# Gated linear attention by 128-token blocks, with the chunks' decays in the queries and their factors made for two heads at once

## The chip, the cores and the metric

The kernel runs on one core of a Trainium2 chip. The time is that of one execution on the device, in microseconds (us); lower is better. All data are float32; products with the large weights are made as three products of float32 parts that were split in two ("h" and "l" tiles).

## The reference

Two layers of an encoder on 272 tokens (16 meta tokens and 256 others), width 1024. In each layer four token mixers run in parallel on one input projection: A (differential attention), B (gated linear attention), C (latent attention), D (windowed attention). Their outputs are gated and merged, and a gated MLP follows. The change lies in mixer B, four heads with 64 key and 128 value channels, run forward and backward over chunks of 64 tokens:

```python
def _gla_direction(q, k, v, log_a):          # v: 128 channels, q and k: 64
    q, k, log_a, v = [by chunks of B_CHUNK = 64]
    b = jnp.cumsum(log_a, axis=2)            # within a chunk
    b_end = b[:, :, -1]
    q_dec = q * jnp.exp(b)
    k_in = k * jnp.exp(-b)
    k_out = k * jnp.exp(b_end[:, :, None] - b)
    att = jnp.einsum('bnthd,bnshd->bnhts', q_dec, k_in) * causal
    o = jnp.einsum('bnhts,bnshe->bnthe', att, v)
    d_state = jnp.einsum('bnshd,bnshe->bnhde', k_out, v)
    def step(S, inp):
        dS, dec = inp
        return dec[..., None] * S + dS, S
    _, S_start = lax.scan(step, S0, (d_state, jnp.exp(b_end)))
    o = o + jnp.einsum('bnthd,nbhde->bnthe', q_dec, S_start)
```

The sum of both directions is normalised over each head's 128 channels and multiplied by a gate. The 272 tokens fall into five chunks: the 16 meta tokens (with padding), and four of 64.

## The kernel before

Activations stand transposed, channels on the 128 partitions and the 272 tokens along the free dimension. A head of mixer B has its 64 forward channels on partitions 0 to 63 and its 64 backward channels on 64 to 127, so that one instruction works on both directions.

The work is written as generators. `interleave(main, n_main, n_fill, fill)` runs `main` step by step and puts `n_fill/n_main` steps of `fill` behind each. In the first stage of a layer `main` is `comp_b1` (decays, with the pair `N_B1`) and then `comp_b2` (the attention itself, `N_B2`), and `fill` is `proj_b_vr` and `proj_a`: projections of the input (tile `pj`), 24 products of 272 columns (258 for some in layer 1) for each block of 128 output channels. Every projection needs its weights split by ScalarE (`wh`, line 221) and by VectorE (`wl`, line 221) from a chunk that arrives by DMA (`raw`); three `raw` and five `wh`/`wl` buffers rotate, the split runs two chunks ahead, and three PSUM banks rotate for `pj`. The framework's scheduler then lays out one fixed order of instructions for each engine; each engine works through its own order and waits by semaphores where an input isn't there.

Mixer B by step, per head h:

- `comp_b1`, first loop: `gpre` (gate logits), Abs, Exp and Ln on ScalarE. Second loop: two scans on VectorE (`x1`), their exponentials on ScalarE (`x3`, `x2`), four small copies of chunk-end decays into `dec` (lines 749 to 752), `ks` and `qs` multiplied with the exponentials, and `ko` (in the tile `x1`): the keys times their chunk's decay (lines 755, 756).
- `keys(h)`: three transposes of `ko` (tile `tk`), copied by ScalarE into `kt` (lines 771, 772).
- `states(h)`: five products `d` (`kt` by values `bvt`), one per chunk, 16 or 64 rows high; two copies and six recursions (line 793) give the state at the start of each chunk, `sst`.
- `scores(h)`: per direction two products of 128 columns and one of 16 (tile `at`, 64 rows high), masks (lines 809, 810) and sums (811, 812) on VectorE, giving `am`.
- `outputs(h)`: `poB`, three products `bvt` by `am` and five `sst` by `qs`, one for each chunk; then squares and `norm(h)` (`ps_B`).

`keys(0)` is the first step of `comp_b2`, `states(0)` the second. The queries of mixer A (`aq`, four blocks) are projected at that time; VectorE reads each block's `pj` (line 544), and ScalarE and VectorE split it (`qmAh`, `qh`, lines 313 and 314).

## Time and profile before

| | |
|---|---|
| median of 3 runs | 1157.58 us (1155.28 to 1157.81) |
| profiled execution, its own time | 1157.4 us |
| its span, first to last instruction | 1155.5 us |
| TensorE matmul busy / weight load busy | 98% / 94% of the span |
| VectorE / ScalarE / GpSimd busy | 82% / 64% / 1% |
| mean granted TensorE clock | 0.997 |

Durations below are of the profiled execution. Matmul rows give start and duration; products follow each other more closely than their durations, so what one costs TensorE is the distance from its start to that of the next. A float32 product that isn't split is recorded as two instructions ("x10" are five products), a split one as one, a transpose as one.

### The profile page before, as it was taken

To read this page: it belongs to the slowest core of one execution; us is meant where nothing else is said; L and a number is where in the kernel's file an instruction comes from. 1 tells how busy PE (TensorE), PEld (TensorE's weight loads), DVE (VectorE), ACT (ScalarE), POOL (GpSimd) and SP (SyncE) were. 2 spreads that over 40 slices of the span, in tenths; PEclk is the share of its full clock that TensorE was granted. 3 is DMA by queue.
4 is the path that set the end of the run, shared out by engine and by line. 5 is a ranking of instruction groups with operands and counts; after the bars stand their busy time and mean duration, and the time that the engine had idled before them with its cause. 6 is when DMAs were issued, how large, how long until landed. Compare 5 with 4: busy or idle time off the path is not lost.

```text
span 1155.5 us, 22869 instructions
## 1 busy us (share of the span) xinstructions
PE 1126.9 (98%) x8686; PEld 1082.9 (94%) x8686; DVE 953.0 (82%) x2153; ACT 743.0 (64%) x1579; POOL 10.5 (1%) x40
## 2 busy tenths in 40 slices
PE   8999999999999999999999999999999999999997
PEld 8989899999999999999999898999999999999986
DVE  7986997898977799995479869978999778999843
ACT  7545886577765767664457447865777657776632
POOL 1000000000000000000000000000000000000000
PEclk9999999999999999999999999999999999999999
DMA  7632454435656356555546424544356463655552
GB/s 261 217 125 92 127 153 144 141 120 142 153 151 201 122 171 201 182 173 168 175 145 220 146 77 125 152 158 152 115 148 169 161 231 102 205 197 191 188 186 74
DMA packets 60914, 183.71 MB, mean 159 GB/s; under 512 B 10443, under 2 KB 17739, under 8 KB 60420
## 3 DMA queue, kind: packets, MB, share of 16 engines
q1 hardware_dynamic: 60148, 181.34, 51.0%
q8 instruction: 68, 1.11, 0.4%
q10 hardware_dynamic: 656, 0.91, 0.2%
q14 instruction: 42, 0.34, 0.1%
HBM read 180.01 MB, written 2.21 MB: 158 GB/s over the span
## 4 chain that ended last, share of the span: by engine, by line
PE 75%; DVE 14%; ACT 5%; issue 3%; DMA 2%; SPq 0%; DVEq 0%; ACTq 0%
PE pj L183 47%; PE dn L183 6%; PE dt L183 5%; PE br L183 5%; DVE wl L221 4%; DMA raw<-wst 2%; ACT wh L221 1%; PE poB L183 1%; PE sc L183 1%; PE at L183 1%; PE poD L183 1%; PE tpp L186 1%; PE d L183 1%; DVE sw L956 1%; PE qu L183 1%
## 5 line engine op out<-in xcount | busy, mean ns | idle before, releaser
L183 PE MATMUL pj<-xh,wh 128*128 128x272 f32 (+1 forms) x1888 | 546.1, 291 | 4.8 <-ACT xh L352 3.9
L183 PE MATMUL pj<-xl,wh 128*128 128x272 f32 (+1 forms) x1888 | 540.4, 287 | 0.0
L183 PE MATMUL pj<-xh,wl 128*128 128x272 f32 (+1 forms) x1888 | 539.8, 287 | 0.0
L221 ACT CAST wh<-raw 128x1024 fp32r<-128x1024 f32 (+2 forms) x322 | 332.7, 1035 | 220.7 <-PE pj L183 94.6
L221 DVE TENSOR_TENSOR wl<-raw,wh 128x1024 fp32r<-128x1024 f32 (+2 forms) x322 | 387.1, 1205 | 96.9 <-ACT wh L221 93.9
L183 PEld LDWEIGHTS pj<-xh,wh 128*128 128x128 f32 x1888 | 354.1, 188 | 10.6 <-ACT xh L352 5.0
L183 PEld LDWEIGHTS pj<-xl,wh 128*128 128x128 f32 x1888 | 356.1, 189 | 1.5 <-issue 0.5
L183 PEld LDWEIGHTS pj<-xh,wl 128*128 128x128 f32 x1888 | 355.7, 188 | 0.4
L1320 ACT ACTIVATE cv<-u,pc 128x272 f32<-128x272 f32 (+1 forms) x88 | 52.8, 605 | 11.3 <-DVE u L1318 11.0
L183 PE MATMUL dn<-ah,wh 128*128 128x272 f32 x176 | 51.0, 290 | 0.0
L183 PE MATMUL dn<-al,wh 128*128 128x272 f32 x176 | 50.7, 288 | 0.0
L183 PE MATMUL dn<-ah,wl 128*128 128x272 f32 x176 | 50.5, 287 | 0.0
L609 ACT ACTIVATE p<-p,st 128x272 f32<-128x272 f32 x68 | 35.1, 517 | 14.8 <-DVE st L607 14.6
L1324 DVE SCALAR_TENSOR_TENSOR cv<-u,pc,cv 128x271 f32<-128x271 f32 (+1 forms) x88 | 43.1, 490 | 1.8
L1322 DVE SCALAR_TENSOR_TENSOR cv<-u,pc,cv 128x271 f32<-128x271 f32 (+1 forms) x88 | 43.0, 488 | 1.2 <-ACT cv L1320 0.9
L1171 DVE TENSOR_TENSOR gt<-pj,rs_x 128x272 f32<-128x272 f32 (+1 forms) x64 | 27.5, 429 | 18.6 <-PE pj L183 18.3
L1318 DVE TENSOR_TENSOR u<-pj,rs_x 128x272 f32<-128x272 f32 (+1 forms) x88 | 37.0, 427 | 0.0
L183 PE MATMUL dt<-wh,al 128*128 128x512 f32 x88 | 34.8, 395 | 0.0
L183 PE MATMUL dt<-wh,ah 128*128 128x512 f32 x88 | 34.7, 395 | 0.0
L183 PE MATMUL dt<-wl,ah 128*128 128x512 f32 x88 | 34.5, 392 | 0.0
L183 PEld LDWEIGHTS dn<-ah,wh 128*128 128x128 f32 x176 | 33.1, 188 | 0.0
L183 PEld LDWEIGHTS dn<-al,wh 128*128 128x128 f32 x176 | 33.1, 188 | 0.0
(385 smaller groups left out, 1922.7 us busy)
## 6 DMA issues: line engine op xcount, KB each, us to landing
raw<-wst SPq DMA_DIRECT2D x306, 512.0 KB, 3.7
raw<-wst SPq DMA_DIRECT2D x12, 384.0 KB, 3.2
bD<-bvec SPq DMA_DIRECT2D x16, 256.0 KB, 5.1
bA<-bvec SPq DMA_DIRECT2D x8, 400.0 KB, 5.4
hT<-hT SPq DMA_DIRECT2D x1, 1088.0 KB, 6.6
h_dram<-hT SPq DMA_DIRECT2D x1, 1088.0 KB
hT<-h_dram SPq DMA_DIRECT2D x1, 1088.0 KB, 6.1
raw<-wst SPq DMA_DIRECT2D x4, 256.0 KB, 4.7
```

Of the source, the lines that this page charges most:

```text
L183: self.note(nc.tensor.matmul(*args, **kw))
L186: self.note(nc.tensor.transpose(*args, **kw))
L221: pair = S.copy(wh[:, c], raw[:, c]), V.tensor_sub(wl[:, c], raw[:, c], wh[:, c].bitcast(F32))
L609: S.activation(p, p, AF.Exp, scale=-1.0, bias=st[:, 0:1], accum_out=st[:, 1:2])
L956: V.tensor_mul(sw[a:a + 32, c0:], src[z:z + 32, c0:], C("sin", z, z + 32)[:, c0:])
L1171: V.tensor_mul(f[:, ct:T], (yield from pj(ct))[:, ct:T], RS[:, ct:T])
L1318: V.tensor_mul(u_[:, ct:T], ps[:, ct:T], RS[:, ct:T])
L1320: S.activation(t[:, cd:T], u_[:, cd:T], AF.Identity, scale=PCc("cw1", c), bias=PCc("cb", c))
L1322: V.scalar_tensor_tensor(t[:, lo:T], u_[:, lo - 1:T - 1], PCc("cw0", c), t[:, lo:T], ALU.mult, ALU.add)
L1324: V.scalar_tensor_tensor(t[:, cd:T - 1], u_[:, cd + 1:T], PCc("cw2", c), t[:, cd:T - 1], ALU.mult, ALU.add)
```

## The change

Mixer B no longer makes a state for each chunk of 64 tokens, but only for each block of 128 (and the meta tokens' block): three blocks instead of five chunks. What lies between the two chunks of a block comes into the scores, and what a chunk's place in its block adds to the decay is multiplied into the queries (`q2`, in the tile `x2`) by a factor `mq`, and into the keys (`kx`, in the tile `x1`) by `mk`. `factors` makes both, with `two` (the decay over a whole block), for two heads at once, in seven small VectorE instructions.

- `comp_b1`: the minimum and the subtraction become one instruction behind the Ln. The `dec` copies go to ScalarE, two a head. `ko` goes; `kx` is made in `keys`. `keys(0)` is called in the step of head 2 and `states(0)` in that of head 3. `N_B1` and `N_B2` give more fill steps per step of `comp_b1`, (8, 24), and as many less to `comp_b2`, (15, 17).
- `states`: three products over 128 rows; two recursions instead of six.
- `scores`: eight products of 64 columns (four with `ks`, four with `kx`), the two directions in turn, and two of 16 columns; one mask product per direction and one sum.
- `outputs`: six products instead of eight: `sst` by `q2`, of 16, 128 and 128 columns.
- GpSimd clears what the higher products now read of `bvt` and `kt`, and sets `mq`, `mk` and a column of `dec`.

```diff
-N_B1, N_B2, N_A, N_CU, N_C, N_D = (8, 22), (17, 19), (24, 30), (7, 14), (19, 24), (35, 36)
+N_B1, N_B2, N_A, N_CU, N_C, N_D = (8, 24), (15, 17), (24, 30), (7, 14), (19, 24), (35, 36)
...
-                    V.tensor_scalar(x1[h], ps[:, :T], 0.0, None, ALU.min)
                     act(LN_EXP_SET, x2[h], x2[h], AF.Exp, scale=-1.0)
                     act(LN_EXP_SET, x2[h], x2[h], AF.Ln, bias=1.0)
+                    V.scalar_tensor_tensor(x1[h], ps[:, :T], 0.0, x2[h], ALU.min, ALU.subtract)
...
+                def factors(hs):
+                    f, b = slice(0, 64), slice(64, 128)
+                    V.tensor_mul(two[:, hs, :], dec[:, hs, 0:4:2], dec[:, hs, 1:4:2])
+                    V.tensor_copy(mk[f, hs, 0::2], dec[f, hs, 1:4:2])
+                    V.tensor_copy(mk[b, hs, 1::2], dec[b, hs, 2::2])
+                    V.tensor_copy(mq[f, hs, 1::2], dec[f, hs, 0:4:2])
+                    V.tensor_copy(mq[f, hs, 2::2], two[f, hs, :])
+                    V.tensor_copy(mq[b, hs, 0:3:2], dec[b, hs, 1:4:2])
+                    V.tensor_copy(mq[b, hs, 1:2], two[b, hs, 1:2])
...
-                    V.tensor_copy(dec[0:64, 0:1], x2[h][0:64, 15:16])
-                    V.tensor_copy(dec[0:64, 1:5], x2[h][0:64, 79::64])
-                    V.tensor_copy(dec[64:128, 0:1], x2[h][64:128, 0:1])
-                    V.tensor_copy(dec[64:128, 1:5], x2[h][64:128, 16:T:64])
+                    S.copy(dec[0:64, h, :], x2[h][0:64, 15::64])
+                    S.copy(dec[64:128, h, 1:5], x2[h][64:128, 16:T:64])
                     V.tensor_mul(ks[h], ks[h], x3)
-                    ko = x1[h]
-                    V.tensor_scalar(ko[:, 0:16], ks[h][:, 0:16], dec[:, 0:1], None, ALU.mult)
-                    V.tensor_mul(ko[:, 16:T].rearrange("p (c t) -> p c t", c=4),
...
                     V.tensor_mul(qs[h], qs[h], x2[h])
+                    if h % 2:
+                        factors(slice(h - 1, h + 1))
+                    if h == 2:
+                        keys(d, 0)
+                    if h == 3:
+                        states(d, 0)
                     yield
...
+            def keys(d, h):
+                V.tensor_mul(by_chunk(kx[:, 16:T]), by_chunk(ks[:, 16:T]),
+                             d["mk"][:, h, :].unsqueeze(2).to_broadcast([P, 4, 64]))
...
+            def states(d, h):
+                for b_ in (0, 2, 1):
+                    PE.matmul(dS[b_], lhsT=kt[:, b_, :], rhs=bvt[:, b_ * P:(b_ + 1) * P], start=True, stop=True)
+                S.copy(sst[0:64, 1, :], dS[0][0:64])
+                S.copy(sst[64:128, 1, :], dS[2][64:128])
+                for r, b_, i in ((slice(0, 64), 2, 0), (slice(64, 128), 0, 1)):
+                    V.scalar_tensor_tensor(sst[r, b_, :], sst[r, 1, :], d["two"][r, h, i:i + 1], dS[1][r], ALU.mult,
+                                           ALU.add)
...
+                        for far in range(2):
+                            for dr, at in enumerate(ats):
+                                c0 = 64 * (far ^ dr)
+                                PE.matmul(at[:, b_ * P + c0:b_ * P + c0 + 64], lhsT=(kx if far else ks)[r2[dr], t0_:t0_ + P],
+                                          rhs=qs[r2[dr], t0_ + c0:t0_ + c0 + 64], start=True, stop=True)
+                    for dr, at in enumerate(ats):
+                        PE.matmul(at[:, 256:272], lhsT=ks[r2[dr], 0:P], rhs=qs[r2[dr], 0:16], start=True, stop=True)
+                    for dr, at in enumerate(ats):
+                        V.tensor_mul(am[dr], at[:, 0:272], C("cmask")[:, 272 * dr:272 * dr + 272])
+                    V.tensor_add(am[0], am[0], am[1])
+                    S.activation(q2[:, 0:16], qs[:, 0:16], AF.Copy, scale=mq[:, 0:1])
+                    V.tensor_mul(by_chunk(q2[:, 16:T]), by_chunk(qs[:, 16:T]),
+                                 mq[:, 1:5].unsqueeze(2).to_broadcast([P, 4, 64]))
...
+                    for c0, n, b_, a0 in ((0, 16, 0, 256), (16, P, 1, 0), (16 + P, P, 2, P)):
+                        PE.matmul(po[:, c0:c0 + n], lhsT=bvt[:, b_ * P:(b_ + 1) * P], rhs=am[:, a0:a0 + n], start=True,
+                                  stop=False)
+                        PE.matmul(po[:, c0:c0 + n], lhsT=sst[:, b_, :], rhs=q2[:, c0:c0 + n], start=False, stop=True)
```

How the change moves instructions is seen in the engines' orders. The first place is TensorE's (PE's) order in layer 0 around the first transposes `tk` of `keys(0)`. Before, they stand behind the third block of mixer A's queries (`pj_863`, read into `aq2`):

```order
L183 MATMUL pj_863<-xh_153,wh_779 128x272
L183 MATMUL pj_863<-xl_154,wh_779 128x272
L183 MATMUL pj_863<-xh_153,wl_780 128x272
L186 MATMUL tk_889<-cc_83,x10_411 16x128
L186 MATMUL tk_889<-cc_83,x10_411 128x128 x2
L183 MATMUL pj_903<-xh_153,wh_812 128x272
```

Of the change, they stand behind the first of these blocks (`pj_774`, read into `aq0`):

```order
L183 MATMUL pj_774<-xh_153,wh_689 128x272
L183 MATMUL pj_774<-xl_154,wh_689 128x272
L183 MATMUL pj_774<-xh_153,wl_690 128x272
L186 MATMUL tk_810<-cc_83,ks0_357 16x128
L186 MATMUL tk_810<-cc_83,x10_411 128x128 x2
L183 MATMUL pj_825<-xh_153,wh_721 128x272
```

So `tk` moved up by two blocks, 48 products. The products `d` of `states(0)` came 12 products behind `tk` before, and come 36 behind it now. In layer 1 the numbers are the same.

The second place is ScalarE's (ACT's) order around the copies into `kt` that lie between `tk` and `d`. Before:

```order
L221 CAST wh_859<-raw_857 128x1024
L221 CAST wh_899<-raw_897 128x1024
L313 CAST qmAh_92<-aq0_776 64x16 x2
L313 CAST qh_1558<-aq0_776 128x256
L221 CAST wh_975<-raw_973 128x1024
L313 CAST qmAh_92<-aq1_809 64x16 x2
L313 CAST qh_1640<-aq1_809 128x256
L221 CAST wh_1046<-raw_1044 128x1024
L771 COPY kt_890<-tk_889 16x128
L772 COPY kt_890<-tk_889 128x256
```

Of the change:

```order
L835 ACTIVATE x23_418<-qs3_356,mq_673 128x16
L221 CAST wh_854<-raw_852 128x1024
L221 CAST wh_914<-raw_912 128x1024
L794 COPY kt_811<-tk_810 16x128
L795 COPY kt_811<-tk_810 128x256
L313 CAST qmAh_92<-aq0_767 64x16 x2
L313 CAST qh_1544<-aq0_767 128x256
L221 CAST wh_977<-raw_975 128x1024
```

The copies moved ahead of the splits of `aq0` and `aq1` and of two weight casts; the two casts that still stand ahead of them are the ones that stood ahead of `aq0` before. In layer 1 it is the same.

The third place is the scores of head 0 in PE's order (layer 0); `at` is a PSUM tile, one for each direction. Before:

```order
L183 MATMUL at_956<-qs0_353,ks0_357 128x128 x2
L183 MATMUL at_956<-qs0_353,ks0_357 16x16
L183 MATMUL at_962<-qs0_353,ks0_357 128x128 x2
L183 MATMUL at_962<-qs0_353,ks0_357 16x16
L183 MATMUL pj_979<-xh_153,wh_859 128x272
```

Of the change:

```order
L183 MATMUL at_955<-qs0_353,ks0_357 128x64
L183 MATMUL at_956<-qs0_353,ks0_357 128x64
L183 MATMUL at_955<-qs0_353,x10_411 128x64
L183 MATMUL at_956<-qs0_353,x10_411 128x64
L183 MATMUL at_955<-qs0_353,ks0_357 128x64
L183 MATMUL at_956<-qs0_353,ks0_357 128x64
L183 MATMUL at_955<-qs0_353,x10_411 128x64
L183 MATMUL at_956<-qs0_353,x10_411 128x64
L183 MATMUL at_955<-qs0_353,ks0_357 128x16
L183 MATMUL at_956<-qs0_353,ks0_357 128x16
```

One direction (partitions 0 to 63) was done whole before the other (64 to 127); now they alternate product by product. From here to the first product of `outputs` PE has 12, 15, 24 and 12 projection products for heads 0 to 3 before, and 18, 14, 21 and 21 now.

## Rows read from the trace of the kernel before

**Rows 1.** The page: busy time of the engines, with share of the span and instructions.

```profile
PE 1126.9 (98%) x8686; PEld 1082.9 (94%) x8686; DVE 953.0 (82%) x2153; ACT 743.0 (64%) x1579; POOL 10.5 (1%) x40
```

**Rows 2.** The waits of PE over the whole span: who waited for whom, us in total, times, longest.

```profile
PE d L183 <- ACT kt L771: 3.3, 2, 1.8
```

**Rows 3.** Timeline of PE in layer 0, from the last projection products ahead of `states(0)` to the next transposes (start, duration, what, [idle before, who ended it]).

```profile
62.03 0.49 PE L186 MATMUL tk<-cc,x 128*16 128x128 f32 x3
...
63.74 0.29 PE L183 MATMUL pj<-xh,wl 128*128 128x272 f32 x1
65.81 1.54 PE L183 MATMUL d<-bvt,kt 16*128 16x128 f32 x10 [1.77 <-ACT kt L771]
...
70.00 0.49 PE L186 MATMUL tk<-cc,x 128*16 128x128 f32 x3
```

**Rows 4.** Stretches of that time, in us: length, busy time (instructions) of each engine, then the granted PE clock, DMA share and GB/s.

```profile
24.00:62.00 38.00, 38.00 (x294) 37.14 (x294) 36.20 (x79) 23.38 (x48) 0.00 (x0) 1.00 0.56 185
...
66.00:70.00 4.00, 4.00 (x23) 3.62 (x23) 3.33 (x9) 0.84 (x5) 0.00 (x0) 0.57 0.83 253
```

**Rows 5.** Timeline of PE in layer 1 around `states(0)`, and `states(1)`.

```profile
643.94 0.49 PE L186 MATMUL tk<-cc,x 128*16 128x128 f32 x3
...
644.39 0.28 PE L183 MATMUL pj<-xl,wh 128*128 128x258 f32 x1
...
645.59 0.28 PE L183 MATMUL pj<-xh,wl 128*128 128x258 f32 x1
647.38 1.13 PE L183 MATMUL d<-bvt,kt 16*128 16x128 f32 x10 [1.50 <-ACT kt L771]
...
649.98 0.49 PE L186 MATMUL tk<-cc,x 128*16 128x128 f32 x3
```

**Rows 6.** Timeline of ACT in layer 0 up to the copies into `kt`.

```profile
57.75 1.99 ACT L221 CAST wh<-raw 128x1024 fp32r<-128x1024 f32 x2
61.52 0.43 ACT L313 CAST qmAh<-aq 64x16 fp32r<-64x16 f32 x2 [1.79 <-DVE aq L544]
...
65.50 0.25 ACT L771 COPY kt<-tk 16x128 f32<-16x128 f32 x1
65.66 0.36 ACT L772 COPY kt<-tk 128x256 f32<-128x256 f32 x1
```

**Rows 7.** Timeline of DVE in layer 0: the last `dec` copy of head 1, and the first query block of mixer A.

```profile
46.95 0.16 DVE L752 COPY dec<-x 64x4 f32<-64x4 f32 x1
...
61.00 0.43 DVE L544 SCALAR_TENSOR_TENSOR aq<-pj,rs_x 128x272 f32<-128x272 f32 x1
```

**Rows 8.** Timeline of ACT in layer 1: the last weight cast ahead of `aq0`.

```profile
639.67 1.05 ACT L221 CAST wh<-raw 128x1024 fp32r<-128x1024 f32 x1 [1.50 <-DMA raw<-wst]
```

**Rows 9.** Timeline of PE in layer 0 for `outputs(0)` and `states(1)`, with the projection products around them.

```profile
72.21 0.29 PE L183 MATMUL pj<-xl,wh 128*128 128x272 f32 x1
...
73.47 0.29 PE L183 MATMUL pj<-xh,wl 128*128 128x272 f32 x1
73.69 0.39 PE L183 MATMUL poB<-am,bvt 16*128 16x16 f32 x2
...
74.25 0.47 PE L183 MATMUL poB<-am,bvt 128*128 128x128 f32 x2
74.56 0.56 PE L183 MATMUL poB<-qs,sst 128*128 128x64 f32 x4
74.95 0.44 PE L183 MATMUL poB<-am,bvt 128*128 128x128 f32 x2
75.22 0.56 PE L183 MATMUL poB<-qs,sst 128*128 128x64 f32 x4
75.59 0.37 PE L183 MATMUL pj<-xh,wh 128*128 128x272 f32 x1
...
77.06 0.29 PE L183 MATMUL pj<-xh,wl 128*128 128x272 f32 x1
77.28 1.13 PE L183 MATMUL d<-bvt,kt 16*128 16x128 f32 x10
78.34 0.39 PE L183 MATMUL pj<-xh,wh 128*128 128x272 f32 x1
```

**Rows 10.** The same for `ps_B` of head 1, which closes the 12 products behind `states(1)`, and for the scores of head 3 in layer 1.

```profile
79.95 0.41 PE L183 MATMUL ps_B<-sq,ones_r 128*128 128x272 f32 x2
...
682.67 1.63 PE L183 MATMUL at<-qs,ks 64*128 64x128 f32 x12
684.23 0.39 PE L183 MATMUL pj<-xh,wh 128*128 128x272 f32 x1
```

**Rows 11.** Groups of PE instructions by shape, from 676 to 692 us (head 3 of layer 1): count, busy us, mean ns. "64*128 64x128" is a product 64 rows high with 128 weight columns and 128 moving ones.

```profile
L183 PE MATMUL at<-qs,ks 64*128 64x128 f32 x8 | 1.4, 297 | 0.0
...
L183 PE MATMUL d<-bvt,kt 64*128 64x128 f32 x8 | 0.7, 297 | 0.0
```

**Rows 12.** Groups of DVE instructions from 24 to 110 us (mixer B of layer 0).

```profile
L793 DVE SCALAR_TENSOR_TENSOR sst<-sst,dec,d 64x128 f32<-64x128 f32 x24 | 8.3, 346 | 3.0 <-ACT sst L789 2.4
L809 DVE TENSOR_TENSOR am<-at,cc 128x256 f32<-128x256 f32 x8 | 3.4, 420 | 1.1 <-PE at L183 1.0
...
L856 DVE SCALAR_TENSOR_TENSOR x<-x,pc,qs 128x272 f32<-128x272 f32 x3 | 1.5, 487 | 0.0
...
L752 DVE COPY dec<-x 64x4 f32<-64x4 f32 x4 | 0.6, 160 | 0.0
```

More of the change, by code (lines that the diff above doesn't have):

```diff
@@ L61 @@
 _n = 0
-for _name, _w in (("ident", 128), ("ones", 128), ("comb", 64), ("cmask", 512), ("smask", 272), ("cos", 272),
+for _name, _w in (("ident", 128), ("ones", 128), ("comb", 64), ("cmask", 544), ("smask", 272), ("cos", 272),
                   ("sin", 272), ("sel0", 1), ("sel1", 1)):
@@ L701, in proj_b_vr @@
                 bvt = [mix.tile([P, 2, 3 * P], F32, name="bvt", tag="bv", bufs=2) for _ in range(2)]
+                for t in bvt:
+                    G.memset(t[:, :, 0:P], 0.0)
                 d["bvt"] = bvt = [bvt[h // 2][:, h % 2, :] for h in range(4)]
@@ L733, in comp_b1 @@
                     S.activation(x2[h], ps[:, :T], AF.Abs)
-                    V.tensor_scalar(x1[h], ps[:, :T], 0.0, None, ALU.min)
                     act(LN_EXP_SET, x2[h], x2[h], AF.Exp, scale=-1.0)
                     act(LN_EXP_SET, x2[h], x2[h], AF.Ln, bias=1.0)
+                    V.scalar_tensor_tensor(x1[h], ps[:, :T], 0.0, x2[h], ALU.min, ALU.subtract)
                     yield
-                d["dec"] = mix.tile([P, 4, 5], F32, name="dec")
+                dec = mix.tile([P, 4, 5], F32, name="dec")
+                two = mix.tile([P, 4, 2], F32, name="two")
+                mq = mix.tile([P, 4, 5], F32, name="mq")
+                mk = mix.tile([P, 4, 4], F32, name="mk")
+                G.memset(mq, 1.0)
+                G.memset(mk, 1.0)
+                d["two"], d["mq"], d["mk"], d["x1"], d["x2"] = two, mq, mk, x1, x2
+                d["parts"] = [{} for _ in range(4)]
+                def factors(hs):
[7 more added lines that the diff above has]
+                    V.tensor_copy(mq[b, hs, 1:2], two[b, hs, 1:2])
+                G.memset(dec[64:128, :, 0:1], 1.0)
                 for h in range(4):
-                    V.tensor_sub(x1[h], x1[h], x2[h])
                     b_ = x1[h][0:64, :]
@@ new lines, in states @@
+            def states(d, h):
+                kt, bvt = d["parts"][h]["kt"], d["bvt"][h]
+                sst = mix.tile([P, 3, P], F32, name="sst", tag="sst", bufs=2)
+                G.memset(sst[0:64, 0, :], 0.0)
+                G.memset(sst[64:128, 2, :], 0.0)
+                dt = axb("d")
+                dS = [dt[:, b_ * P:(b_ + 1) * P] for b_ in range(3)]
+                for b_ in (0, 2, 1):
[5 more added lines that the diff above has]
+                                           ALU.add)
+                d["parts"][h]["sst"] = sst
@@ L811, in scores @@
-                    V.tensor_add(am[0][:, 0:256], am[0][:, 0:256], am[1][:, 0:256])
-                    V.tensor_add(am[0][:16, 256:272], am[0][:16, 256:272], am[1][:16, 256:272])
+                    ats = [scb("at"), scb("at")]
+                    r2 = [slice(0, 64), slice(64, 128)]
+                    for b_ in range(2):
+                        t0_ = 16 + 128 * b_
+                        for far in range(2):
[3 more added lines that the diff above has]
+                                          rhs=qs[r2[dr], t0_ + c0:t0_ + c0 + 64], start=True, stop=True)
@@ L813, in scores @@
                     parts[h]["am"] = am[0]
                 def outputs(h):
[L816 removed]
+                    am, sst, bvt, q2 = parts[h]["am"], parts[h]["sst"], d["bvt"][h], d["x2"][h]
                     po = axb("poB")
[L818 to L819 removed]
@@ L820, in outputs @@
-                    for b_ in range(2):
-                        t0_ = 16 + 128 * b_
-                        PE.matmul(po[:, t0_:t0_ + P], lhsT=bvt[:, (1 + b_) * P:(2 + b_) * P],
-                                  rhs=am[:, b_ * P:b_ * P + P], start=True, stop=False)
-                        for cc_ in range(2):
-                            c = 1 + 2 * b_ + cc_
-                            s0 = 16 + 64 * (c - 1)
-                            PE.matmul(po[:, s0:s0 + 64], lhsT=sst[:, c, :], rhs=qs[:, s0:s0 + 64], start=False,
-                                      stop=cc_ == 1)
@@ L1388, in _constants @@
     s, t = np.meshgrid(np.arange(P), np.arange(P), indexing="ij")
-    same = (s // 64) == (t // 64)
-    mf = (same & (s <= t)).astype(np.float32)
-    mb = (same & (s >= t)).astype(np.float32)
-    put("cmask", np.concatenate([mf, mf, mb, mb], axis=1))
+    masks = []
+    for m in ((s <= t).astype(np.float32), (s >= t).astype(np.float32)):
+        masks += [m, m, np.where(s < 16, m, 0.0)[:, :16]]
+    put("cmask", np.concatenate(masks, axis=1))
     sk = np.ones((P, T))
```

75 lines of the change are left out of this document (19 added, 56 removed).

## The prediction

> **What bounds the kernel now.** First the page's busy line: PE has matmuls in flight for 98% of the span and its weight loads run 94%, DVE is busy 82%, ACT 64% [rows 1]. So PE is the bound, in two ways: what its products cost one after the other, and the few places where it stands still. DVE and ACT count only where they are late for a PE instruction. Second, PE's waits: the wait of `d` for ACT's copies into `kt` is 3.3 us, twice in the run, once a layer [rows 2]. It lies in mixer B, whose code changes. Third, the timeline at these two places.
>
> In layer 0 the last projection product starts at 63.74 and the first `d` at 65.81 [rows 3]. Without a wait the distance is 0.22 (77.06 to 77.28, [rows 9]), so 2.07 - 0.22 = 1.85 us are lost. From there to the next transposes, 65.81 to 70.00, one `states` and 12 products take 4.19 [rows 3]; the same work undisturbed takes 2.67 (77.28 to 79.95, [rows 9, 10]). The granted clock was 0.57 from 66 to 70, after 1.00 up to the wait [rows 4]: most of this stretch ran at 1.2 instead of 2.4 GHz. That is 1.52 more, 3.37 in all. In layer 1 the wait costs 647.38 - 645.59 - 0.22 = 1.57, and the work behind it takes 649.98 - 647.38 = 2.60, nothing lost to the clock [rows 5]. **Both together: 4.94 us.**
>
> Why `kt` is late: ACT works in order. Its copies at 65.50 stood behind the splits of `aq0` and `aq1`, and the first of these waited until 61.52 for DVE, which read `aq0` only at 61.00 [rows 6, 7]. DVE was busy 36.2 of the 38 us before [rows 4]; ACT inherits its backlog, and PE inherits it from ACT.
>
> **The change part by part. The waits.** `tk` moves up by 48 products. Eleven rows from 72.21 to 73.47 [rows 9] give 0.126 a product, so `tk` comes at 62.03 - 6.05 = 56.0 [rows 3]. Three things have to be there.
> First `kx` of head 0: DVE makes it behind the decays of heads 0 and 1, which are ready in `dec` at 47.1 now [rows 7]; seven small instructions (0.16 each, [rows 12]), head 2's scans and some waiting for ACT, which copies `dec` now, may take 4 us more and still leave 4.
> Second `kt`: only two weight casts remain ahead of it, those that ended at 59.74 [rows 6]. If they come no earlier than now, the copies (65.50 to 66.02, so 0.52, [rows 6]) end at 60.3. `d` is due 36 products (4.54) and the transposes (0.49, [rows 3]) behind 56.0, at 61.0. Slack 0.7. In layer 1 a product takes 0.12 (644.39 to 645.59, ten products, [rows 5]): `tk` at 638.2, `d` at 643.0, the cast ahead of `kt` ends at 640.72 [rows 8], the copies at 641.2. Slack 1.8. DVE's backlog itself stays, since before `aq0` it loses about as much work as it gains; only `kt` no longer stands behind it. I take both waits as gone: **-4.9**, bounds 0 and -4.9.
> Third, what is late next: the bank of `aq0` is read at 61.0 and needed again three blocks after its end, at about 63.5. That holds.
>
> **The products**, for each of eight heads. `states`: five products take 77.28 to 78.34, 1.06 [rows 9]. Three of full height and 128 columns take 0.31 or 0.27 each at the pace of `poB` (74.25 to 74.56, 74.95 to 75.22), so 0.87: -0.19. `outputs`: 73.69 to 75.59, 1.90; the two pairs of 64 columns (74.56 to 74.95, 75.22 to 75.59, 0.39 and 0.37) become products of 128 at 0.27 to 0.31: -0.2 [rows 9]. `scores`: now 682.67 to 684.23, 1.56 for six products [rows 10]; of the change ten, so twenty instructions. A `poB` instruction of 64 columns costs 0.0975 (four in 0.39, [rows 9]), hardly less than one of 128 columns, and twenty in a row would cost 1.95 plus about 0.4 for getting in and out: 2.4. But eight instructions of `d` with alternating halves kept PE busy for 0.7 us, eight of `at` of the same shape, one half after the other, for 1.4 [rows 11]: upper and lower half run at once when they alternate. The change alternates all of them, so ten pairs, 1.0 + 0.4 = 1.4: -0.16.
> The Trainium skill ("TensorE: Matmul & The Clock Gate", section on LDWEIGHTS) says that loading weights takes time by their columns, whatever the rows; by that alone, without pairing, the ten products with 128 weight columns each would make `scores` dearer, which is the second rival below. The trace agrees as far as one half goes: 0.0975 for 64 moving columns is hardly less than for 128 [rows 9].
> Sum -0.55 a head, **-4.4** for eight. Bounds per head: `states` -0.47 (six instructions at 0.0975) to -0.1 (all at 0.31), `outputs` -0.37 (the four of 128 columns at 0.0975 an instruction) to 0, `scores` -0.64 (pairs at half of 0.0975) to +0.85 (no pairing): -12 to +6 in all. I take the middle values, since [rows 9, 11] are products of the same kind in the same place.
>
> **What lies beside.** DVE loses, per head, four of six recursions (0.35 each, [rows 12]), 0.6 of `dec` copies, one instruction of two in front of the scans and four small ones at the masks, and gains the query product (0.42) and its share of the factors (0.5): about -2 us a head, but PE doesn't wait for DVE there, so nothing. ACT gains some 0.75 a head, behind its 36% idle time; without that cover it would be the 6 us of eight heads. GpSimd's clears run on an engine that is 1% busy.
> One place is tight: `poB` waits for the masks. They can start only when both `at` are finished, and three instructions of 0.42 plus, for heads 1 and 2, one of 0.49 put between [rows 12] make some 1.75; there are 14, 18 or 21 products ahead (14: 1.76). For head 1 I add 0.1 per layer: **+0.2**.
>
> Sum against the profiled execution's own time, 1157.4 (0.2 under the median, which changes nothing): 1157.4 - 4.9 - 4.4 + 0.2 = **1148.3 us**.
>
> **The rivals.** *A wait in the place of the one removed.* The second cast ahead of `kt` needs the buffer of `aq0`'s weights, free only when `tk` is issued, and a `raw` chunk from DMA; in layer 1 the cast waited 1.50 us for DMA [rows 8]. If half of the 4.9 stays there, or PE arriving 3 us earlier waits for something later in mixer A, the time is 1150.8; if all of it stays, 1153.2. Chance 0.22.
> *The halves don't pair.* Then `scores` is 2.4 instead of 1.56, +6.7 for eight; with the waits and the other products -4.9 - 3.1 + 0.2 the time is 1156.3, within 0.2% of before. For it: these products are shorter than those of `d`, and 16-column ones of 128 weights stand behind them. Against: [rows 11]. Chance 0.07.
> *Slower: the masks become the wait.* If a weight split of DVE (1.2 us) gets in front of the masks whenever both `at` end together, PE waits about 1 us in `outputs` of every head, and if the clock falls to its lower level after it, as in [rows 4], 1.5 more: 8 x 2.5 = 20, minus 9.1, 1168. It decides from 1.1 us a head. Against it: 14 to 21 products of cover, where before 12 were enough without a wait. Chance 0.06.
> *Nothing gained:* the waits stay and products cost the same: 1157. Chance 0.05.
>
> **How the numbers follow.** Forecast 0.60, with its own range 1145 to 1151 (`scores` and `states` between their bounds' middle thirds). The range for 8 in 10 takes in the first rival and a better pairing: 1143.5 to 1155. A measurement of this kernel can tell about 0.2%, 2.3 us. Faster (below 1155.3): the forecast, the first rival and a part of the second, 0.85. Same: the rest of the second and the fourth, 0.09. Slower: 0.06.
>
> **What would show it.** In the profile after: no wait of `d` for `kt` over 0.3 us in either layer, and a granted clock of 1.00 in the stretch behind `states(0)`; `at` from its first instruction to the next projection product at 1.2 to 1.6 us, not 2.4; `d` at 0.8 to 0.95, `poB` at 1.6 to 1.8; DVE busy some 15 us less. I am wrong if `kt` is still late behind the casts, if `poB` has a new wait for `am`, or if PE shows new waits in mixer A that eat the gain.

## The result, and the profile after

| | before | after |
|---|---|---|
| median of 4 runs each, on one chip | 1157.69 us | 1144.80 us (1144.29 to 1145.40) |
| ratio, 95% interval | | 0.9898 (0.9879 to 0.9917) |
| profiled execution; its span | 1157.4; 1155.5 us | 1145.0; 1143.2 us |
| mean granted TensorE clock | 0.997 | 0.999 |

The kernel is 1.0% faster. The forecast was 1148.3 us, 3.5 us above the median, with a range of 1143.5 to 1155 that holds it; the forecast's own narrower range, 1145 to 1151, is missed by 0.2.

The page's busy line answers [rows 1]:

```profile
PE 1116.1 (98%) x8686; PEld 1076.8 (94%) x8686; DVE 938.1 (82%) x2085; ACT 746.3 (65%) x1603; POOL 13.5 (1%) x58
```

VectorE has 14.9 us less to do, as forecast; TensorE loses 10.8 us of busy time. The waits of PE (who waited for whom, us in total, times, longest) answer [rows 2]. No line for `d` and `kt` is left. The last two of these lines are new, the first was 2.2 before:

```profile
PE tpr L186 <- ACT aq L935: 2.0, 2, 1.3
...
PE sc L183 <- DVE ql L314: 1.2, 2, 0.8
PE pj L183 <- DVE r L542: 1.2, 2, 1.0
```

PE's timeline in layer 0 answers [rows 3, 9] (start, duration, what): `states(0)`, then scores and outputs of head 0.

```profile
61.17 0.29 PE L183 MATMUL pj<-xh,wl 128*128 128x272 f32 x1
61.30 0.83 PE L183 MATMUL d<-bvt,kt 128*128 128x128 f32 x6
61.88 0.37 PE L183 MATMUL pj<-xh,wh 128*128 128x272 f32 x1
...
66.92 0.44 PE L183 MATMUL at<-qs,ks 64*128 64x64 f32 x4
...
68.15 0.39 PE L183 MATMUL pj<-xh,wh 128*128 128x272 f32 x1
...
70.40 0.29 PE L183 MATMUL pj<-xh,wl 128*128 128x272 f32 x1
70.52 0.37 PE L183 MATMUL poB<-am,bvt 128*128 128x16 f32 x2
...
71.86 0.37 PE L183 MATMUL pj<-xh,wh 128*128 128x272 f32 x1
```

`d` now takes 61.88 - 61.30 = 0.58 us (before 1.06), `at` 68.15 - 66.92 = 1.23 (1.56), `poB` 71.86 - 70.52 = 1.34 here and 1.26 in most other heads (1.90). `d` and `poB` also start 0.13 and 0.12 behind the projection product ahead of them; before it was 0.22 [rows 9].

The stretch of time behind `states(0)` answers [rows 4]: the granted clock stays at 1.00, its upper level of 2.4 GHz.

```profile
62.00:66.00 4.00, 4.00 (x34) 4.00 (x33) 3.92 (x9) 2.71 (x8) 0.21 (x1) 1.00 0.77 249
```

Where the 12.3 us of span went is read from four marks of PE's timeline. Mixer B ends, and mixer A begins, at the first `scm`; mixer A ends at the first `ps_c`. First the kernel before, then the one after, layer 0 and layer 1:

```profile
115.78 0.28 PE L183 MATMUL scm<-akh,qmAh 128*128 128x272 f32 x1
...
180.93 0.39 PE L183 MATMUL ps_c<-sq,cc 128*128 128x272 f32 x1
...
695.73 0.28 PE L183 MATMUL scm<-akh,qmAh 128*128 128x272 f32 x1
...
760.20 0.39 PE L183 MATMUL ps_c<-sq,cc 128*128 128x272 f32 x1
```

```profile
106.37 0.28 PE L183 MATMUL scm<-akh,qmAh 128*128 128x272 f32 x1
...
174.11 0.62 PE L183 MATMUL ps_c<-sq,cc 128*128 128x272 f32 x2
...
682.25 0.28 PE L183 MATMUL scm<-akh,qmAh 128*128 128x272 f32 x1
...
748.07 0.39 PE L183 MATMUL ps_c<-sq,cc 128*128 128x272 f32 x1
```

In layer 0, 9.41 us are gained by the first `scm` (115.78 to 106.37), and only 6.82 of them are left at `ps_c`: mixer A, which the diff doesn't touch, takes 67.74 us instead of 65.15. Layer 1 begins 6.6 ahead (its first `gpre` at 604.98 instead of 611.55), is 13.48 ahead at `scm` and 12.13 at `ps_c`. So mixer B gains 9.4 + 6.9 = 16.3 us, nearly twice the forecast's 9.1, and mixer A gives 2.6 + 1.35 = 3.95 back.

Three questions follow. Was the wait removed for the reason given? Why did the products save so much more? Why does mixer A lose?

### The profile page after: what moved, and what is told of

Its sections match the earlier page's. It is cut to its first block, busy times and chain, and to the rows that moved or that the text cites. A ratio compares the mean times of both kernels' runs of the same rounds, so it can differ in the third digit from the quotient of the medians.

```text
span 1143.2 us, 22842 instructions
## 1 busy us (share of the span) xinstructions
PE 1116.1 (98%) x8686; PEld 1076.8 (94%) x8686; DVE 938.1 (82%) x2085; ACT 746.3 (65%) x1603; POOL 13.5 (1%) x58
## 4 chain that ended last, share of the span: by engine, by line
PE 78%; DVE 10%; ACT 6%; DMA 3%; issue 2%; SPq 0%; DVEq 0%; ACTq 0%
PE pj L183 50%; PE dn L183 6%; PE br L183 6%; PE dt L183 5%; DVE wl L221 3%; DMA raw<-wst 3%; ACT wh L221 2%; PE sc L183 1%; PE poD L183 1%; PE poB L183 1%; PE at L183 1%; PE tpp L186 1%; DVE sw L972 1%; PE qu L183 1%; ACT p L609 1%
```

## The experiments

Each kernel is compared with the kernel before on the same chip (1156.6 us in the first eight, 1155.5 in the last two). "Ratio" is to that kernel, with its 95% interval.

**The order alone**, in the kernel before:

```
-N_B1, N_B2 = (8, 22), (17, 19)
+N_B1, N_B2 = (8, 24), (15, 17)
...
                     V.tensor_mul(qs[h], qs[h], x2[h])
+                    if h == 2:
+                        keys(d, 0)
+                    if h == 3:
+                        states(d, 0)
...
```

> The kernel before, with one part of the change alone: keys(0) and states(0) are called in the steps of heads 2 and 3 of comp_b1, and the pairs are (8, 24) and (15, 17); products, decays and masks are those of before. Theory: both waits of d for kt go, and with the one in layer 0 the stretch at 1.2 GHz behind it, so 4.9 us: 1157.4 - 4.9 = 1152.5, and nothing else, since the five d products a head, poB and at cost what they did. In PE's order the groups of sc in mixer A stand as before (six behind each other, but for one pair of three), so mixer A should take what it took. Rival: PE arrives earlier and waits for something else; then 1155 to 1157, with a new wait of over 1 us on PE in mixer A or at the evacuations of r.

Measured: 1155.96 us, ratio 0.9999 (0.9987 to 1.0011): no gain. The theory falls, and the rival's place is wrong too. PE's waits, and the stretch behind the new one in layer 0:

```profile
PE poB L183 <- DVE am L817: 2.3, 2, 1.2
...
71.00:76.00 5.00, 5.00 (x29) 4.74 (x28) 2.15 (x6) 1.28 (x3) 0.40 (x2) 0.66 0.30 114
```

`d` no longer waits for `kt`, but the first `poB` of each layer waits for `am`, which VectorE makes, and in layer 0 the clock falls behind that wait as it did behind the old one (0.66 between 71 and 76). VectorE's backlog was not removed. It was collected by the next instruction of PE that needs VectorE.

**The rest of the change without the order**: the changed kernel, with the two calls and the pairs of before.

```
-N_B1, N_B2 = (8, 24), (15, 17)
+N_B1, N_B2 = (8, 22), (17, 19)
...
-                    if h == 2:
-                        keys(d, 0)
-                    if h == 3:
-                        states(d, 0)
...
+                keys(d, 0)
+                yield
                 for h in range(4):
+                    states(d, h)
+                    yield
                     if h:
-                        states(d, h)
-                        yield
```

> The changed kernel without its new order: keys(0) and states(0) are the first steps of comp_b2 again, with the pairs (8, 22) and (17, 19). Theory: the waits of d for kt come back, some 1.6 to 1.8 us a layer, and in layer 0 the slow stretch behind, so 4.9 in all; the products stay as cheap as in the changed kernel: 1144.9 + 4.9 = 1149.8. Rival: the products of before were dear only because of the waits around them, and the change's gain is mostly the order; then 1153 or more.

Measured: 1146.11 us, ratio 0.9912 (0.9896 to 0.9927). Neither the theory's 1149.8 nor the rival's 1153: nearly the whole gain is there without the order. The wait for `kt` is almost gone:

```profile
PE pj L183 <- DVE r L542: 1.3, 2, 0.8
...
PE d L183 <- ACT kt L790: 0.3, 1, 0.3
```

So the gain doesn't need the move. That the work taken from VectorE removed the wait, this run alone doesn't show. In layer 0 `kt` is copied only 0.4 us earlier than before (65.12 against 65.50 [rows 6]), while PE comes to the transposes 1.8 us later (63.82 against 62.03 [rows 3]), having waited on its way 0.8 us at the first `gpre` and 0.5 for VectorE to read `r`:

```profile
63.82 0.27 PE L186 MATMUL tk<-cc,ks 128*16 128x128 f32 x1
...
65.12 0.25 ACT L790 COPY kt<-tk 16x128 f32<-16x128 f32 x1
```

Two runs test VectorE's work from both sides.

**The kernel before, with less work for VectorE.**

```
-                    V.tensor_scalar(x1[h], ps[:, :T], 0.0, None, ALU.min)
                     act(LN_EXP_SET, x2[h], x2[h], AF.Ln, bias=1.0)
+                    V.scalar_tensor_tensor(x1[h], ps[:, :T], 0.0, x2[h], ALU.min, ALU.subtract)
...
-                    V.tensor_sub(x1[h], x1[h], x2[h])
...
-                    V.tensor_copy(dec[0:64, 0:1], x2[h][0:64, 15:16])
-                    V.tensor_copy(dec[0:64, 1:5], x2[h][0:64, 79::64])
-                    V.tensor_copy(dec[64:128, 0:1], x2[h][64:128, 0:1])
-                    V.tensor_copy(dec[64:128, 1:5], x2[h][64:128, 16:T:64])
+                    S.copy(dec[0:64, :], x2[h][0:64, 15::64])
+                    S.copy(dec[64:128, 0:1], x2[h][64:128, 0:1])
+                    S.copy(dec[64:128, 1:5], x2[h][64:128, 16:T:64])
```

> The kernel before with its own order and its own products; only VectorE's work in comp_b1 is cut, as the change cuts it: minimum and subtraction are one instruction behind the Ln, and the chunk-end copies into dec go to ScalarE (three a head). That is some 1.0 us less of VectorE a head, 4 us by the time that it reads aq0. Theory, formed from the two runs order_only (order moved, no gain, and PE waits for am instead) and products_only (order not moved, wait for kt nearly gone): the wait of d for kt was VectorE's backlog, and the change removed it by making VectorE's work less; then the waits fall from 3.3 us to under 0.7, the stretch at 1.2 GHz goes, and the time is 1156.6 - 4.5 = 1152. Rival: the wait needs the move as well (ScalarE has more to do now and is as late with kt); then d waits over 1 us in each layer and the time is 1156.

Measured: 1153.22 us, ratio 0.9962 (0.9945 to 0.9980), less by 4.4 us (by the ratio; 3.4 by the medians), as the theory says. No wait of `d` for `kt` is left. VectorE reads `aq0` three microseconds earlier than in [rows 7], `kt` is copied 1.9 us earlier than in [rows 6] while PE comes to the transposes 0.3 later than before (62.35), and the clock stays at 1.00 in the stretch of [rows 4] (timelines of VectorE and ScalarE, and the stretch):

```profile
57.95 0.42 DVE L544 SCALAR_TENSOR_TENSOR aq<-pj,rs_x 128x272 f32<-128x272 f32 x1
...
63.57 0.25 ACT L769 COPY kt<-tk 16x128 f32<-16x128 f32 x1
...
66.00:70.00 4.00, 4.00 (x32) 3.49 (x32) 3.62 (x14) 1.87 (x5) 0.00 (x0) 1.00 0.31 123
```

**The changed products in the old order (the kernel of products_only), with VectorE's work put back.**

```
-                    V.scalar_tensor_tensor(x1[h], ps[:, :T], 0.0, x2[h], ALU.min, ALU.subtract)
+                    V.tensor_scalar(x1[h], ps[:, :T], 0.0, None, ALU.min)
...
+                    V.tensor_sub(x1[h], x1[h], x2[h])
...
-                    S.copy(dec[0:64, h, :], x2[h][0:64, 15::64])
-                    S.copy(dec[64:128, h, 1:5], x2[h][64:128, 16:T:64])
+                    V.tensor_copy(dec[0:64, h, :], x2[h][0:64, 15::64])
+                    V.tensor_copy(dec[64:128, h, 1:5], x2[h][64:128, 16:T:64])
                     V.tensor_mul(ks[h], ks[h], x3)
+                    V.tensor_mul(x3, x3, x3)
```

> The kernel of products_only (1146.1) with VectorE's work in comp_b1 put back: minimum and subtraction apart, the copies into dec on VectorE, and for each head one product of 272 columns whose result nobody reads, in place of the keys' product of before. Some 1.0 us a head more. Theory: VectorE is late for aq0 again, d waits for kt by 1 us or more in each layer, and in layer 0 a stretch at the lower clock follows: 1146.1 + 4 = 1150. Rival: VectorE's load doesn't decide; the time stays at 1146 with a wait under 0.5.

Measured: 1152.47 us, ratio 0.9961 (0.9948 to 0.9975): 6.4 us more than products_only (5.7 by the ratios), in the theory's direction and more than its 4. `V.tensor_mul(x3, x3, x3)` is the product whose result nobody reads. Its wait of PE:

```profile
PE d L183 <- ACT kt L792: 5.6, 2, 3.0
```

In layer 0 the wait is 2.59 us. `kt` is copied 1.35 us later than in products_only (66.47 against 65.12), and PE is ready for `d` 1.5 earlier (64.18 against 65.66), without the waits for `gpre` and `r`. So the length of the wait is only in part VectorE's; the longer time is the firmer sign. With light_dve both sides agree: the wait for `kt` goes and comes with VectorE's work in `comp_b1`.

**The order once more**, in a kernel with mixer A settled (a_paired, below) and the two calls and the pairs of before:

```
-N_B1, N_B2 = (8, 24), (15, 17)
+N_B1, N_B2 = (8, 22), (17, 19)
...
```

> The kernel of a_paired (1139.9) with keys(0) and states(0) back at the start of comp_b2 and the pairs (8, 22) and (17, 19), as in products_only. It prices the moved order once more, with mixer A's order the same in both kernels. Theory: with VectorE's work cut, the wait for kt is gone in either order (0.3 us in products_only), so the order is worth little: 1139.9 + 1 = 1141, within 2 us of a_paired. Rival: the gain of the order hid in mixer A's varying order, and it is worth the 4.9 us that the wait cost before: 1145.

Measured: 1141.71 us, ratio 0.9876 (0.9861 to 0.9890), 1.8 us above a_paired (2.3 by the ratios); products_only against the changed kernel was 1.3 (1.6). The intervals of both pairs overlap, so the order is worth between nothing and some 2 us, and not the 4.9 of the wait.

**The rows' height**, in the changed kernel:

```
+                    n = P if b_ else 16
-                    PE.matmul(dS[b_], lhsT=kt[:, b_, :], rhs=bvt[:, b_ * P:(b_ + 1) * P], start=True, stop=True)
+                    PE.matmul(dS[b_], lhsT=kt[:n, b_, :], rhs=bvt[:n, b_ * P:(b_ + 1) * P], start=True, stop=True)
...
+                        m = P if b_ else 16
-                        PE.matmul(po[:, c0:c0 + n], lhsT=bvt[:, b_ * P:(b_ + 1) * P], rhs=am[:, a0:a0 + n], start=True,
+                        PE.matmul(po[:, c0:c0 + n], lhsT=bvt[:m, b_ * P:(b_ + 1) * P], rhs=am[:m, a0:a0 + n], start=True,
```

> The changed kernel, but the first product of states and the first of outputs read only the 16 rows that hold meta tokens, as before the change, in place of 128 rows of which the rest is zero. No other instruction changes. Theory: in the two traces a product whose weights have another shape than those ahead starts 0.22 behind them instead of 0.126, and the one after it 0.23 instead of 0.12; going to 16 rows and back is paid twice, about 0.35 us for d and as much for poB: 0.7 a head, 5.6 for eight, 1150.5, with d at about 1.0 us and poB at 1.8 us. Rival: only columns cost, rows don't: then d and poB stay at 0.66 and 1.41 and the time at 1145.

Measured: 1150.50 us, ratio 0.9948 (0.9933 to 0.9963), 5.7 us more than the changed kernel's 1144.8, as the theory says. PE's timeline for `outputs(0)` and `states(1)` of layer 0:

```profile
71.70 0.29 PE L183 MATMUL pj<-xh,wl 128*128 128x272 f32 x1
71.92 0.39 PE L183 MATMUL poB<-am,bvt 16*128 16x16 f32 x2
...
73.38 0.38 PE L183 MATMUL pj<-xh,wh 128*128 128x272 f32 x1
...
74.09 0.29 PE L183 MATMUL pj<-xh,wl 128*128 128x272 f32 x1
74.31 1.12 PE L183 MATMUL d<-bvt,kt 16*128 16x128 f32 x6
75.19 0.37 PE L183 MATMUL pj<-xh,wh 128*128 128x272 f32 x1
```

The same six instructions of `d` take 0.88 instead of 0.58, `poB` 1.46 instead of 1.26, and each starts 0.22 behind the projection product instead of 0.12 to 0.13. That is 0.30 + 0.20 + 2 x 0.09 = 0.68 a head, 5.4 for eight; the price expected for a head, 0.7, was right, but `d` and `poB` themselves stay below the 1.0 and 1.8 named. Around `d` the change between 16 and 128 rows costs TensorE about 0.1 us in the first and in the second instruction at each end: the first four of the six follow what is ahead of them by 0.22, 0.21, 0.20 and 0.21, and by 0.12, 0.11, 0.11 and 0.11 in the changed kernel. The Trainium skill ("TensorEngine Tiling (Array Packing)", section on Key Properties) says that changing the tiling mode drains TensorE. The extra 0.1 us at each change of height fit that and give a size here; that a drain is their cause no row shows.

**The halves one after the other**, in the changed kernel:

```
-                    for b_ in range(2):
-                        t0_ = 16 + 128 * b_
-                        for far in range(2):
-                            for dr, at in enumerate(ats):
-                                c0 = 64 * (far ^ dr)
+                    for dr, at in enumerate(ats):
+                        for b_ in range(2):
+                            t0_ = 16 + 128 * b_
+                            for far in range(2):
+                                c0 = 64 * (far ^ dr)
...
-                    for dr, at in enumerate(ats):
                         PE.matmul(at[:, 256:272], lhsT=ks[r2[dr], 0:P], rhs=qs[r2[dr], 0:16], start=True, stop=True)
```

> The changed kernel, but scores issues the ten products of the forward direction (rows 0 to 63) and then the ten of the backward direction (rows 64 to 127), instead of one of each in turn: four of 64 columns and one of 16 for a direction, each recorded as two instructions. Theory: upper and lower half run at once only where they are issued in turn, so at takes twice 10 instructions at 0.105 instead of ten pairs: from 1.15 to about 2.2 us a head, 8.4 us for eight, 1153. Rival: TensorE starts the second direction on its half while the first is still running, as the trace of before shows it for sc in mixer A (118.89: three products of rows 0 to 63 and then three of rows 64 to 127 in PE's order, yet their starts are 10 ns apart); then at stays at 1.1 to 1.3 us and the time at 1145.

Measured: 1149.74 us, ratio 0.9944 (0.9928 to 0.9961), 4.9 us more than the changed kernel: between theory and rival. PE's timeline for the scores of head 0:

```profile
66.92 0.43 PE L183 MATMUL at<-qs,ks 64*128 64x64 f32 x2
...
67.64 0.32 PE L183 MATMUL at<-qs,ks 64*128 64x64 f32 x1
...
68.86 0.40 PE L183 MATMUL pj<-xh,wh 128*128 128x272 f32 x1
```

`at` takes 68.86 - 66.92 = 1.94, 0.71 more than in turn (5.7 for eight). The second direction starts at 67.64, while three more instructions of the first are still to start: the halves overlap at the seam, some four instructions deep, and no further. Issuing them in turn is what makes all of them overlap.

**The scores of the kernel before in turn, and nothing else.**

```
-                    for dr in range(2):
-                        at = scb("at")
-                        r = slice(64 * dr, 64 * dr + 64)
-                        for b_ in range(2):
-                            t0_ = 16 + 128 * b_
-                            PE.matmul(at[:, b_ * P:b_ * P + P], lhsT=ks[r, t0_:t0_ + P], rhs=qs[r, t0_:t0_ + P],
+                    ats = [scb("at"), scb("at")]
+                    r2 = [slice(0, 64), slice(64, 128)]
+                    for b_ in range(2):
+                        t0_ = 16 + 128 * b_
+                        for dr, at in enumerate(ats):
+                            PE.matmul(at[:, b_ * P:b_ * P + P], lhsT=ks[r2[dr], t0_:t0_ + P], rhs=qs[r2[dr], t0_:t0_ + P],
...
```

> The kernel before, but scores issues its six products with the two directions in turn (two pairs of 128 columns and one of 16) and the masks behind them. Everything else as before, the waits for kt too. In TensorE's order the sc products of mixer A's first heads then stand as in the changed kernel: apart from each other, in groups of three with projections between. Theory: at goes from 1.56 to about 0.95 us a head, 4.9 for eight; mixer A gives some of it back, as in the changed kernel (its sc groups took 1.4 and 0.9 us longer in the two layers than before, and their turns more): 3 to 4; 1156.6 - 4.9 + 3.5 = 1155. Rival: mixer A's loss in the changed kernel has another cause (its earlier start), then it isn't here and the time is 1151.7.

Measured: 1156.81 us, ratio 0.9999 (0.9984 to 1.0014). The theory's side, and further than it said: `at` falls to 0.79 us in four of the eight heads (in three of the others projections stand between its instructions, and the first still runs behind the wait for `kt`, at a granted clock of 0.57). Mixer A is longer by 2.95 us in layer 0 and 1.48 in layer 1 (first `scm` to first `ps_c`, as above), which is more than the 2.6 and 1.35 of the changed kernel, though in layer 0 it begins only 1.8 us earlier. The rival, an earlier start as the cause, falls.

**Mixer A's halves together.** In mixer A a head's scores for a block of queries are six products `sc`, three with rows 0 to 63 and three with rows 64 to 127. PE's timeline of the first such group, before and then after:

```profile
118.89 0.40 PE L183 MATMUL sc<-akh,qh 64*128 64x272 f32 x2
...
119.47 0.39 PE L183 MATMUL pj<-xh,wh 128*128 128x272 f32 x1
```

```profile
109.48 0.39 PE L183 MATMUL sc<-akh,qh 64*128 64x272 f32 x1
...
109.98 0.39 PE L183 MATMUL sc<-akh,qh 64*128 64x272 f32 x1
...
110.55 0.39 PE L183 MATMUL pj<-xh,wh 128*128 128x272 f32 x1
```

Before, the two halves ran at once: 119.47 - 118.89 = 0.58 us for six products. After, the second half begins when the first has ended: 1.07. The next groups of layer 0 are split by projections. The order of PE shows the same split in pairs_only, low_rows, unpaired, products_only and loaded_dve, which all write the two directions' `at` tiles together, and the order of before in order_only and light_dve, which don't: mixer A of layer 0 takes 67.6 to 68.1 us in the first five and 65.2 to 65.8 in the other two. The experiment, in `comp_a` of the changed kernel (`read[0]` is the last reciprocal that the softmax of an earlier block put into VectorE's order):

```
-                        pp = []
-                        for m in range(2):
-                            r = slice(64 * m, 64 * m + 64)
-                            qr = slice(128 - 128 * qt, 256 - 128 * qt)
-                            ps = scb("sc")
-                            mm3(ps[:, :T], qh[r, qr], ql[r, qr], ak[0][h][r, :], ak[1][h][r, :], True, True)
+                        pp, pss, last = [], [scb("sc"), scb("sc")], read[0]
+                        qr = slice(128 - 128 * qt, 256 - 128 * qt)
+                        for i in range(3):
+                            for m in range(2):
+                                r = slice(64 * m, 64 * m + 64)
+                                mm = nc.tensor.matmul(pss[m][:, :T], lhsT=(qh, qh, ql)[i][r, qr], rhs=ak[i % 2][h][r, :],
+                                                      start=i == 0, stop=i == 2)
+                                PE.note(mm)
+                                order(mm, last)
+                                last = mm
...
```

> The changed kernel, with one thing in mixer A: the two halves' sc products (rows 0 to 63 and 64 to 127) of a query block are written in turn, and an issue order puts the first of them behind the softmax of the block before, so that both banks are free when they start and no projection comes between them. Theory: what mixer A lost is that halves no longer ran at once; all eight groups of a layer now take 0.58 us: sc falls from 6.99 to 4.6 us in layer 0 and from 6.41 to 4.6 in layer 1, 4.2 in all, and with some seven turns fewer about 5: 1140. Rival: the groups start later than they did, and what follows in mixer A (tpr, which waits for ScalarE's aq) is later by as much; then 1145 or more, with longer waits on tpr.

Measured: 1139.91 us, ratio 0.9856 (0.9836 to 0.9876): 4.9 us less than the changed kernel, the fastest here. The theory's time holds. Groups of PE's `sc` instructions in mixer A of layer 0 (count, busy us, mean ns), of the changed kernel and of this one:

```profile
L183 PE MATMUL sc<-akh,qh 64*128 64x272 f32 x16 | 4.4, 390 | 0.0
L183 PE MATMUL sc<-akh,ql 64*128 64x272 f32 x16 | 3.3, 296 | 0.4 <-DVE ql L314 0.4
L183 PE MATMUL sc<-akl,qh 64*128 64x272 f32 x16 | 3.2, 285 | 0.0
```

```profile
L926 PE MATMUL sc<-akh,qh 64*128 64x272 f32 x16 | 3.1, 389 | 0.0
L926 PE MATMUL sc<-akl,qh 64*128 64x272 f32 x16 | 2.3, 284 | 0.0
L926 PE MATMUL sc<-akh,ql 64*128 64x272 f32 x16 | 2.3, 282 | 0.0
```

The same 48 instructions of the same duration keep TensorE busy for 7.7 us instead of 10.9, because every one overlaps another. Mixer A now takes 64.48 us in layer 0 and 64.49 in layer 1 (before 65.15 and 64.47, after 67.74 and 65.82), so the whole loss is back. The wait of `tpr`, the rival's, shrank from 2.0 to 0.9 us in the whole run.

Not all of the loss was overlap, though. PE's waits inside mixer A of layer 0, first before, then in the changed kernel:

```profile
PE tpr L186 <- ACT aq L919: 0.3, 1, 0.3
```

```profile
PE tpr L186 <- ACT aq L935: 1.3, 1, 1.3
```

With the wait for `ql` (0.4, above) and two smaller ones they grew from 0.7 to 1.9 us, 1.2 of the 2.6 lost there; in layer 1 they fell from 2.4 to 1.7. In a_paired none of 0.2 us or more is left in layer 0. And a_paired overlaps more than the kernel before did, where the same 48 instructions are busy for 9.7 us. So it shows what the new order of `sc` is worth, 4.9 us, and not that lost overlap was all that mixer A had lost.

**The copies of the decays**, in the kernel of a_paired:

```
-                    S.copy(dec[0:64, h, :], x2[h][0:64, 15::64])
-                    S.copy(dec[64:128, h, 1:5], x2[h][64:128, 16:T:64])
+                    V.tensor_copy(dec[0:64, h, :], x2[h][0:64, 15::64])
+                    V.tensor_copy(dec[64:128, h, 1:5], x2[h][64:128, 16:T:64])
```

> The kernel of a_paired with one thing more: the two copies a head into dec are VectorE's again, not ScalarE's. In the changed kernel a projection waits 1.0 us in layer 1 for VectorE to read r, which stands behind seven factor instructions, two products and the keys' product in VectorE's order. Theory: VectorE has 0.3 us a head more to do ahead of the same reads, so the wait for r and that of d for kt stay or grow: 1140 to 1142. Rival: VectorE was held up by ScalarE's copies, which stand behind 1.0 us casts; then the wait for r goes, and the time is 1138.5.

Measured: 1143.57 us, ratio 0.9893 (0.9874 to 0.9912). The rival falls; the theory's sign is right, and its price was too low: 3.7 us for 16 copies. The wait of a projection for `r` doubled, from 1.2 in a_paired:

```profile
PE pj L183 <- DVE r L542: 2.2, 2, 1.5
```

About one of the 3.7 us lies ahead of that, at the first `gpre` (27.17 instead of 26.05), where the copies have no part yet, so at most 2.6 are the copies'.

## Why the prediction was right or wrong

**The waits: right in size, wrong in the step that removes them.** Both waits and the slow stretch went, and light_dve prices them alone at 4.4 us by its ratio against the forecast's 4.9. But the prediction had `kt` come earlier because it "no longer stands behind" VectorE's backlog, and said that the backlog itself "stays, since before `aq0` it loses about as much work as it gains". The first half alone gains nothing (order_only): PE then waits for `am` behind the same backlog. The second half is the wrong step. VectorE reads `aq0` at 59.59 in the changed kernel, 1.4 us earlier than in [rows 7], and light_dve and loaded_dve show that a microsecond a head on VectorE decides. The changed kernel's lines, with the last step of `am` of head 0:

```profile
59.59 0.43 DVE L544 SCALAR_TENSOR_TENSOR aq<-pj,rs_x 128x272 f32<-128x272 f32 x1
...
69.93 0.44 DVE L834 TENSOR_TENSOR am<-am 128x272 f32<-128x272 f32 x1
```

That the changed kernel doesn't wait for `am` has a second reason. `am` is done at 70.37 there, 2.2 us behind the scores, and 18 projection products cover that; order_only has 12 in this place, as the kernel before has. With 12 PE would have waited some 0.6 us (an estimate: 68.15, 12 x 0.126 and 0.13 make 69.79). No run here parts the two reasons.

Of the waits the prediction asked only whether the one for `kt` would be gone. It is, and that alone would have confirmed the wrong cause.

**The products: direction right, size off by a factor of 2.6.** The forecast was -0.55 a head. Measured: `states` -0.48 (forecast -0.19), `outputs` -0.63 (-0.2), `scores` -0.33 (-0.16), together -1.44, and 0.19 more at the two entries, for which the sum had no term: -1.63 a head, 13 us for eight. The mis-sized step is the choice of 0.27 to 0.31 us for a full product of 128 columns, read from `poB` in [rows 9]. Those rows stand among products of other shapes, and the prediction itself called 0.0975 for 64 columns "hardly less" than for 128, which 0.135 to 0.155 an instruction is not. In `d` after, six instructions take 0.58, so a product costs 0.19; the lower bound, 0.0975 an instruction, was the right row. For `outputs` even the bound that it gave, -0.37, is passed, since the product of 16 rows, which the sum left as it was, got cheaper too. That is what low_rows shows: in the changed kernel a stay at 16 rows in `d` costs 0.39 us on top, twice what the padded product itself takes, and GpSimd's clears, which the prediction costed at nothing, buy back 5.7 us of the 13.

**The pairing: right.** `at` takes 1.23, inside the 1.2 to 1.6 named, against 1.94 without alternation, so the rival of unpaired halves (2.4) was priced too high, since halves overlap at the seam anyway.

**What is late next: missed.** The rival in which PE "waits for something later in mixer A" named the place, and in layer 0 waits are 1.2 us of what is lost there; over both layers they are only some 0.5 of the 3.95. What it didn't name is lost overlap: the `sc` groups take 1.4 and 0.9 us longer (0.4 of that is a wait for `ql`). Some 1.5 us of the 3.95 stay open. A second small one lies in `comp_b1`: a projection waits for `r` (1.2 us in all), which in layer 1 stands in VectorE's order behind seven factor instructions, two products and the keys' product. The term of 0.2 for the masks has nothing to show for it: no wait of `poB` for `am` is in the list.

The sum as it turned out, from the profiled executions: waits -4.9 (as the rows of before price them), products and entries -13.0, new waits for `r` +1.2, mixer A +3.95, together -12.75, against 1145.0 - 1157.4 = -12.4. The forecast had -9.1; its errors of +8.6 on the products and about -5 on what is given back hid each other, which is why the total looks better than its terms.

## What to carry to other kernels

When an engine waits at the end of a chain that begins with another engine's backlog, moving the last link can move the wait to that engine's next consumer; ask which work leaves the backlogged engine, and test the cause by adding and removing that work. Products that use half of the rows are cheap only next to products on the other half, and each change of shape has a price at both ends, so padding a 16-row product with zeros can be the faster form. After any edit that changes the order of a neighbour's instructions, compare the stages that the diff doesn't touch.

## What was not expected of the hardware

Halves can overlap without being issued in turn: three instructions each in mixer A of the kernel before (0.58 us for six products), the last four or so of ten in unpaired. They don't always: the next group of six in the kernel before takes 0.93 us (121.69 to 122.62). Where the second half is held back until the first has ended, the overlap is lost (1.07); what held it in the changed kernel isn't named by the trace, and a_paired changed two things there at once, the issue order and the projections in between.

A wait doesn't always cost the clock its upper level. In layer 0 a wait of 1.77 us was followed by a granted clock of 0.57 [rows 4] and one of 1.1 us in order_only by 0.66, but in loaded_dve, where PE stood still for 2.59 us ahead of `d`, the stretch behind it reads 1.00. In layer 1 of the same run, behind 3.02 us, it reads 0.66:

```profile
66.77 0.49 PE L183 MATMUL d<-bvt,kt 128*128 128x128 f32 x2 [2.59 <-ACT kt L792]
...
66.00:70.00 4.00, 3.23 (x29) 3.03 (x31) 3.91 (x12) 2.55 (x8) 0.21 (x1) 1.00 0.42 139
...
646.00:650.00 4.00, 4.00 (x25) 3.81 (x27) 3.91 (x11) 1.48 (x6) 0.21 (x1) 0.66 0.44 135
```

Why one wait is followed by the lower level and another isn't stays open; the 1.5 us for it in the sum of the waits is a property of that place, not a rule.
